# Turning part of the probability tiles by DMA in a two-layer attention trunk, with three score banks and a reordered gate projection

## The chip, the cores and the metric

The kernel runs on one core of one Trainium2 chip. The metric is device time in microseconds (us) of one execution. The profile and the trace are of one profiled execution.

## The reference: what is computed

Two layers on x of 1024 tokens by 1024 features, all in float32. Each layer normalises x, multiplies it with one wide input matrix whose columns hold all queries, keys, values and gates, runs two kinds of attention, multiplies each output with silu of its gate, and adds a final projection to x.

- Layer 1: attention A (8 heads, 2 key groups) sees the 256 keys that a separate small score picks for each query; attention B (8 heads, 2 key groups) sees a window of 128 keys and a sink.
- Layer 2: attention C (8 heads, 2 key groups) is a gated sum of three attentions: over compressed keys, over selected blocks (all 16 blocks are taken at this length, so it is causal), and over a window of 512. Attention D (8 heads) has queries and keys from low-rank latents, and is causal.

```python
def layer_ab(x, ...):
    y = rms_norm(x, norm_g) @ w_in
    qa, ka, va, qi, ki, wi, za, qb, kb, vb, zb = split_cols(y, AB_SPLITS)
...
    mix = jnp.concatenate([oa * jax.nn.silu(za), ob * jax.nn.silu(zb)], axis=-1)
    return x + mix @ w_out
```

Layer 2 has the same shape with C and D in place of A and B.

## The kernel before, in words

**Stages.** Queries go in tiles of 128 rows. The order of the stages, with their place in the profiled execution: normalising, first projections and the small scores (0 to about 165 us); a search in 2 x 16 steps for each query's threshold on VectorE, ScalarE and GpSimd (`topk`, L868), with the jobs of attention B beside it (to about 445); attention A (to about 600); the output projection of layer 1, normalising, and the first projections of layer 2 (to about 800); attention C, first key group 0, then 1, with the other projections beside it (to about 1215); keys and values of D, then attention D, key group 0, then 1, and the output tiles (to the end).

**Numbers.** Projections and scores are made as sums of products of a high and a low part (three or two matmuls each). Probabilities are also split: a high and a low 16-bit part.

**A job** (`attn_gen`, L617) is one query tile, one key group (4 heads) and, in C, one of three kinds. It is done in **units**: a unit is one pass over 4 heads when there are up to 2 key tiles, 2 heads for 3 or 4 key tiles, and 1 head for more. For each unit:
1. scores on TensorE into a PSUM bank `psS` (L665); the masked minimum of the negative on VectorE into `pt` (L668), the bias on ScalarE (L672), and the exponential with its sum on ScalarE (L674). `pt` has three buffers.
2. The probabilities must be turned (keys to partitions) before they can be multiplied with the values. The tiles of a unit are taken in groups of up to four. How a group is turned is given by a letter that cycles through `WAYS` (L73), with one entry for each kind of attention and key group. **p**: TensorE turns the tiles into a bank `psT` (L709), ScalarE copies the high part out (L712), VectorE subtracts for the low part (L713). **q**: the same turn, ScalarE copies all into `sg` (L716), and GpSimd makes both parts (L717, L718). **g**: ScalarE copies `pt` to 16 bits into `hl` (L693), GpSimd subtracts (L694), and a DMA transpose on SP's queue turns both halves at once into `ht` (L696); TensorE has no turn to do. Before, only B uses "g".
3. Three matmuls for each tile with the values, into the bank `psO` (L725 to L727). After a job's last group, `fin` scales the sum and stores it (L788 and L791, or L1337 to L1344 for C).

**The order of the work.** The turning stage and the value stage are closures in two queues, `tq` and `cq`. After the scores of a unit are written out, turning stages are taken from `tq` until only `tlag` of them (L782: the number of groups in this unit) are left, and a value stage is taken from `cq` when there is more than one.
Projections run beside the jobs: `Lanes.run` (L152) adds up costs that the two generators yield, and hands out projection steps (`fill_gen`, L495) up to a ratio of the attention's cost. Chunks of projections go in the order of the strings `FAO` (layer 1) and `FOO` (layer 2); a chunk of queries waits at its gate (L484) until one of three query buffers is free. Shorter chains (normalising, rotating and turning of queries and keys) are posted and go one step at each tick; one of them at a time may hold a `psT` bank. On top of that order, a scheduler of the framework that models the engines' times puts the instructions of each engine in a queue, with waits in between.

**PSUM** has eight banks: two `pp` for projections, two `psS` for scores, three `psT` for turned tiles, one `psO`. **Buffers:** `hl` (the tag under which `sg` also goes) and `ht` have four each (L41, L42).

**SP's queue** issues all loads and stores, in order, the DMA transposes among them.

## Time and profile before

| what | value |
|---|---|
| median of 3 runs | 1537.46 us (1534.99 to 1539.63) |
| profiled execution | 1541.3 us |
| its span, first to last instruction | 1539.1 us |
| mean granted TensorE clock | 0.950 |
| TensorE busy | 1355.2 us (88%) |
| VectorE busy | 1126.2 us (73%) |
| ScalarE busy | 940.5 us (61%) |
| GpSimd busy | 856.1 us (56%) |
| DMA, share of 16 engines | 22.9% |

In the rows, PE is TensorE (PEld its weight loads, which overlap its matmuls), DVE is VectorE, ACT is ScalarE, POOL is GpSimd, SP is SyncE. L709 is line 709 of the kernel. A busy share is an average over stages with different limits, so rows are read by stretch.

### The profile page before, as it was taken

To read this page: it belongs to the slowest core of one execution; us is meant where nothing else is said; L and a number is where in the kernel's file an instruction comes from. 1 tells how busy PE (TensorE), PEld (TensorE's weight loads), DVE (VectorE), ACT (ScalarE), POOL (GpSimd) and SP (SyncE) were. 2 spreads that over 40 slices of the span, in tenths; PEclk is the share of its full clock that TensorE was granted. 3 is DMA by queue.
4 is the path that set the end of the run, shared out by engine and by line. 5 is a ranking of instruction groups with operands and counts; after the bars stand their busy time and mean duration, and the time that the engine had idled before them with its cause. 6 is when DMAs were issued, how large, how long until landed. Compare 5 with 4: busy or idle time off the path is not lost.

```text
span 1539.1 us, 34696 instructions
## 1 busy us (share of the span) xinstructions
PE 1355.2 (88%) x12468; PEld 1244.8 (81%) x12468; DVE 1126.2 (73%) x3401; ACT 940.5 (61%) x2683; POOL 856.1 (56%) x1158
## 2 busy tenths in 40 slices
PE   5998899796268899999999999999998678789999
PEld 5997889695266788999999988899987557678887
DVE  5387888888888774185276678776699999986763
ACT  5355588788668763164246668747677677655541
POOL 6799549987466584225355334465455465742240
PEclk9999999998579999999899999999999879989999
DMA  6311373331131433142212110111100120111232
GB/s 201 91 30 34 73 143 78 75 63 52 35 101 47 111 92 112 44 157 61 54 29 79 46 29 6 29 53 49 33 7 30 59 61 14 35 62 63 93 114 76
DMA packets 120236, 100.83 MB, mean 66 GB/s; under 512 B 52992, under 2 KB 104960, under 8 KB 120064
## 3 DMA queue, kind: packets, MB, share of 16 engines
q1 hardware_dynamic: 120064, 98.62, 22.9%
q8 instruction: 98, 1.61, 0.4%
q14 instruction: 74, 0.61, 0.1%
HBM read 67.65 MB, written 23.07 MB: 59 GB/s over the span
## 4 chain that ended last, share of the span: by engine, by line
PE 49%; DVE 23%; ACT 9%; DMA 7%; POOL 6%; issue 6%; SPq 1%; POOLq 0%; DVEq 0%; ACTq 0%
PE pp L519 8%; PE pp L521 8%; PE pp L520 8%; PE psS L665 6%; PE psT L709 5%; DVE pt L668 4%; ACT pt L674 3%; ACT junka L885 2%; DMA wraw<-in_ab_w_in 2%; PE pp L1732 2%; PE pp L1734 2%; PE pp L1733 2%; DVE ht L713 1%; DVE junk L889 1%; PE po L727 1%
## 5 line engine op out<-in xcount | busy, mean ns | idle before, releaser
L519 PE MATMUL pp<-whi,Rh 128*128 128x256 f32 (+4 forms) x1648 | 480.4, 292 | 15.5 <-DVE zst L610 6.2
L521 PE MATMUL pp<-whi,Rl 128*128 128x256 f32 (+4 forms) x1648 | 475.5, 289 | 0.0
L520 PE MATMUL pp<-wlo,Rh 128*128 128x256 f32 (+4 forms) x1648 | 473.8, 288 | 1.1 <-POOL wlo L476 1.1
L519 PEld LDWEIGHTS pp<-whi,Rh 128*128 128x128 f32 x1648 | 315.5, 192 | 21.9 <-DVE zst L610 6.6
L520 PEld LDWEIGHTS pp<-wlo,Rh 128*128 128x128 f32 x1648 | 316.0, 192 | 3.1 <-POOL wlo L476 1.6
L521 PEld LDWEIGHTS pp<-whi,Rl 128*128 128x128 f32 x1648 | 315.6, 192 | 1.3
L674 ACT ACTIVATE pt<-pt,nm 128x256 f32<-128x256 f32 (+8 forms) x384 | 244.3, 638 | 3.5
L476 POOL TENSOR_TENSOR wlo<-wraw,whi 128x256 fp32r<-128x256 f32 (+4 forms) x208 | 162.8, 792 | 137.8 <-ACT whi L475 136.8
L709 PE MATMUL psT<-identf,pt 128*128 128x128 f32 x1136 | 195.9, 284 | 13.3 <-ACT pt L674 3.5
L475 ACT ACTIVATE whi<-wraw 128x256 fp32r<-128x256 f32 (+4 forms) x208 | 83.3, 416 | 134.7 <-DMA wraw<-in_ab_w_in 41.0
L709 PEld LDWEIGHTS psT<-identf,pt 128*128 128x128 f32 x1136 | 131.9, 143 | 28.0 <-ACT pt L674 8.5
L717 POOL TENSOR_SCALAR ht<-sg 128x512 f16<-128x512 f32 (+3 forms) x127 | 70.0, 552 | 142.0 <-ACT sg L716 108.5
L712 ACT ACTIVATE ht<-psT 128x512 f16<-128x512 f32 (+3 forms) x233 | 112.5, 493 | 57.2 <-PE psT L709 50.5
L713 DVE TENSOR_TENSOR ht<-psT,ht 128x512 f16<-128x512 f32 (+3 forms) x233 | 128.4, 558 | 18.3 <-ACT ht L712 17.4
L725 PEld LDWEIGHTS <-ht 128*128 128x128 f16 x1256 | 117.0, 100 | 26.2 <-DMA ht<-hl 8.4
L727 PEld LDWEIGHTS <-ht 128*128 128x128 f16 x1256 | 115.5, 100 | 26.8 <-POOL ht L718 8.8
L718 POOL TENSOR_TENSOR ht<-sg,ht 128x512 f16<-128x512 f32 (+3 forms) x127 | 127.3, 1003 | 7.2
L668 DVE CUSTOM_DVE_ANT_0 pt<-psS,mk 128x512 f32<-128x512 f32 (+4 forms) x208 | 107.5, 521 | 28.7 <-PE psS L665 22.7
L726 PEld LDWEIGHTS <-ht 128*128 128x128 f16 x1256 | 117.3, 100 | 2.1 <-issue 0.9
L672 ACT ACTIVATE nm<-nm 128x1 f32<-128x1 f32 (+2 forms) x208 | 41.9, 202 | 100.6 <-DVE nm L668 99.8
L716 ACT ACTIVATE sg<-psT 128x512 f32<-128x512 f32 (+3 forms) x127 | 66.7, 526 | 27.7 <-PE psT L709 26.7
L1093 POOL TENSOR_TENSOR mo<-mo,nz 128x256 f32<-128x256 f32 (+1 forms) x32 | 32.4, 1012 | 78.6 <-DMA nz<-zdr 49.6
(314 smaller groups left out, 3695.2 us busy)
## 6 DMA issues: line engine op xcount, KB each, us to landing
wraw<-in_cd_w_in SPq DMA_DIRECT2D x72, 128.0 KB, 2.1
wraw<-in_ab_w_in SPq DMA_DIRECT2D x56, 128.0 KB, 2.3
xs<-in_x SPq DMA_DIRECT2D x8, 512.0 KB, 6.2
od<-mx SPq DMA_DIRECT2D x32, 128.0 KB, 1.8
wraw<-in_ab_w_out SPq DMA_DIRECT2D x32, 128.0 KB, 2.2
x<-in_x SPq DMA_DIRECT2D x8, 512.0 KB, 5.0
mo<-od SPq DMA_DIRECT2D x16, 256.0 KB, 2.8
nz<-zdr SPq DMA_DIRECT2D x16, 256.0 KB, 3.0
```

What stands on the lines that cost most here:

```text
L476: G.tensor_tensor(lo[:, :o], raw[:, :o], hi[:, :o].bitcast(F32), OP.subtract)
L519: T.matmul(ps, xh, hi[:, :n], start=q == 0 and k == 0, stop=False)
L520: T.matmul(ps, xh, lo[:, :n], start=False, stop=False)
L521: T.matmul(ps, xl, hi[:, :n], start=False, stop=q == 3 and k == 1)
L668: V.tensor_tensor_reduce(pt[:, j * nk + c:j * nk + c + w], ps[:, at:at + w], mask(c, w), -1.0, first, op0=OP.add, op1=OP.min, accum_out=low)
L674: S.activation(pt[:, j * nk:(j + 1) * nk], pt[:, j * nk:(j + 1) * nk], AF.Exp, scale=-1.0, bias=nm[:, h:h + 1], accum_out=sm[:, h:h + 1])
L709: T.transpose(pT[:, a], pt[:, o:o + P], identf)
L713: V.tensor_tensor(pl, pT[:, :n], ph, OP.subtract)
L718: G.tensor_tensor(pl, sg[:, :n], ph, OP.subtract)
L725: T.matmul(dst, ph[:, a], vh(kt, h), start=kt == 0, stop=False)
L726: T.matmul(dst, ph[:, a], vl(kt, h), start=False, stop=False)
L727: T.matmul(dst, pl[:, a], vh(kt, h), start=False, stop=kt == nt - 1)
```

## The change

- In jobs of C's selected and windowed kinds and of D, the first group of up to four tiles of every unit but the job's last is turned by DMA, with a new letter "l": the split of "g", with its values multiplied not in its own turn but after the values of the next unit of the job. Such a group has no turning stage in `tq`.
- The other groups of C and D all go the way "p" (before: "ppq", "pq", "ppq" and "p").
- Tiles that TensorE turns go to a buffer of their own, `hp`, with four buffers; `hl` and `ht` have two each.
- The start and stop flags of the value matmuls are set once for the whole output bank, by a count, in place of once a head.
- Three banks for scores and two for turned tiles.
- The gate projection `z2` comes ahead of both chunks of A's (masked) queries.

```diff
-HLB = 4
-HTB = 4
+HLB = 2
+HTB = 2
+HPB = 4
...
-FAO = 'ki qi kb qb0 z0 z1 qb1 ka qa0 z2 qa1'
+FAO = 'ki qi kb qb0 z0 z1 qb1 ka z2 qa0 qa1'
...
-WAYS = ('g', 'g', 'ppq', 'pq', 'ppq', 'pq', 'ppq', 'p')
+WAYS = ('g', 'g', 'ppq', 'pq', 'p', 'p', 'p', 'p')
...
-    psA = {n: ctx.enter_context(tc.tile_pool(name=n, bufs=2, space=PSUM)) for n in ("pp", "psS")}
-    psT = ctx.enter_context(tc.tile_pool(name="psT", bufs=3, space=PSUM))
+    psA = {n: ctx.enter_context(tc.tile_pool(name=n, bufs=2, space=PSUM)) for n in ("pp",)}
+    psA["psS"] = ctx.enter_context(tc.tile_pool(name="psS", bufs=3, space=PSUM))
+    psT = ctx.enter_context(tc.tile_pool(name="psT", bufs=2, space=PSUM))
...
+            heads = [0]
+
+            def values(grp, ph, pl, get_po=get_po, heads=heads, nk=nk, vh=vh, vl=vl, cmp_=cmp_):
+                po = get_po()
+                nt = max(1, nk // P)
+                for a, (h, kt, o) in enumerate(grp):
+                    dst = po[:, h:h + 2].rearrange("p h d -> p (h d)") if cmp_ else po[:, h]
+                    T.matmul(dst, ph[:, a], vh(kt, h), start=heads[0] == 0, stop=False)
+                    T.matmul(dst, ph[:, a], vl(kt, h), start=False, stop=False)
+                    heads[0] += 1
+                    T.matmul(dst, pl[:, a], vh(kt, h), start=False, stop=heads[0] == (2 if cmp_ else 4 * nt))
...
+                u += 1
                 for c in range(0, len(todo), 4):
                     n = min(4, len(todo) - c)
-                    way.append(next(jb["way"]))
+
+                    way.append("l" if c == 0 and jb.get("late") and h0 + per < 4 else next(jb["way"]))
                     ht = None
-                    if way[-1] in "dg":
+                    if way[-1] in "dgl":
...
+                    if way[-1] == "l":
+                        late.append((u, lambda values=values, g=todo[:n], ht=ht, n=n: values(g, ht[:, :n], ht[:, n:2 * n])))
                     turned.append(ht)
                 for c in range(0, len(todo), 4):
+                    if way[c // 4] == "l":
+                        continue
...
                         if way in "pq":
-                            ht = wk.tile([P, 8, P], F16, name="ht", bufs=HTB)
+                            ht = wk.tile([P, 8, P], F16, name="hp", bufs=HPB)
...
+                            values(grp, ph, pl)
+                            k = n
+                            while endu and late and late[0][0] < u:
+                                late.pop(0)[1]()
+                                k += 4
+                            if endu and fb is not None:
                                 assert fb
-                                fin(po, fb[0])
-                            return n * 87 + (0 if not lastg else 1)
+                                fin(get_po(), fb[0])
+                            return k * 87 + (0 if not endu else 1)
```

## Rows read from the trace of the kernel before

**Rows 1.** Busy time by stretch: start:end length, engines, clock, DMA share, GB/s
```profile
350.00:445.00 95.00, 42.40 (x320) 37.62 (x319) 78.80 (x189) 60.73 (x149) 54.95 (x52) 0.64 0.25 63
445.00:600.00 155.00, 138.01 (x1636) 119.06 (x1635) 113.98 (x325) 115.81 (x300) 101.12 (x128) 1.00 0.31 92
900.00:1000.00 100.00, 93.73 (x1088) 82.23 (x1089) 81.32 (x303) 74.96 (x233) 41.52 (x57) 0.98 0.05 15
1000.00:1100.00 100.00, 99.85 (x1023) 97.34 (x1022) 67.93 (x243) 61.38 (x204) 55.44 (x75) 1.00 0.16 46
1100.00:1245.00 145.00, 116.16 (x1217) 101.70 (x1216) 133.85 (x541) 100.77 (x328) 83.65 (x125) 0.91 0.10 32
1245.00:1380.00 135.00, 108.44 (x976) 93.37 (x975) 126.99 (x385) 93.29 (x255) 81.77 (x104) 0.92 0.15 47
1380.00:1524.00 144.00, 143.81 (x1155) 121.48 (x1155) 94.04 (x268) 66.35 (x174) 39.13 (x50) 1.00 0.26 85
```

**Rows 2.** Chain of waits by line: 850-1000, 1100-1245, 1380-1524, 1245-1380
```profile
by line: PE psT L709 13.7%; PE psS L665 11.9%; ACT pt L674 10.4%; PE pp L520 7.0%; PE pp L521 7.0%; PE pp L519 6.9%; issue 6.7%; DVE pt L668 4.6%; DMA wraw<-in_cd_w_in 4.2%; PE po L727 3.4%; PE po L725 3.2%; PE po L726 3.1%; DVE ht L713 2.4
...
by line: DVE pt L668 10.9%; ACT pt L674 6.9%; PE psT L709 6.7%; PE psS L665 5.3%; issue 4.5%; DVE kd L1539 4.5%; DVE ht L713 4.4%; DVE rs_t L310 3.7%; DVE rs_t L312 2.7%; DVE rs_y L313 2.7%; DVE ydup L1436 2.5%; DVE rs_t L309 2.4%; DVE rs_t
...
by line: PE pp L1732 17.4%; PE pp L1734 16.8%; PE pp L1733 16.7%; PE psS L665 15.1%; PE psT L709 10.0%; PE psT L1100 3.2%; PE po L725 3.0%; PE po L727 2.9%; PE po L726 2.8%; PE psT L1669 1.9%; PE psT L1686 1.9%; DMA mo<-od 1.9%; PE psT L112
...
by line: DVE pt L668 13.7%; DVE ht L713 6.5%; PE psS L665 6.4%; DVE rs_v L306 4.3%; DVE qrs L1691 4.2%; issue 4.1%; PE psT L709 3.5%; DVE kd L1539 2.5%; ACT pt L674 2.5%; DVE nz L1654 2.3%; DVE rs_t L309 2.3%; DVE qhl L1673 2.3%; PE psT L16
```

**Rows 3.** Turns on TensorE: their group (busy, mean ns), a chain piece
```profile
L709 PE MATMUL psT<-identf,pt 128*128 128x128 f32 x1136 | 195.9, 284 | 13.3 <-ACT pt L674 3.5 <-DVE ht L713 2.5 <-ACT sg L716 2.2
...
941.88 1.09 PE psT L709 x8
```

**Rows 4.** Turned groups: L713, L716 from 1100 to 1245 (ns); then whole span
```profile
L713 DVE TENSOR_TENSOR ht<-psT,ht x34: 276/552/692, 1102.9 to 1213.7; 128x512 f16<-128x512 f32 x16, 128x128 f16<-128x128 f32 x12, 128x384 f16<-128x384 f32 x4, 128x256 f16<-128x256 f32 x2
...
L716 ACT ACTIVATE sg<-psT x34: 267/578/637, 1103.6 to 1212.3; 128x512 f32<-128x512 f32 x20, 128x128 f32<-128x128 f32 x8, 128x256 f32<-128x256 f32 x6
...
L717 POOL TENSOR_SCALAR ht<-sg 128x512 f16<-128x512 f32 (+3 forms) x127 | 70.0, 552 | 142.0 <-ACT sg L716 108.5 <-ACT nm L672 30.4 <-DVE ht L713 1.7
...
L718 POOL TENSOR_TENSOR ht<-sg,ht 128x512 f16<-128x512 f32 (+3 forms) x127 | 127.3, 1003 | 7.2
...
L693 ACT ACTIVATE hl<-pt 128x512 f16<-128x512 f32 x30 | 17.7, 619 | 0.0
...
L694 POOL TENSOR_TENSOR hl<-pt,hl x30: 1145/1167/3132, 182.7 to 434.6; 128x512 f16<-128x512 f32 x30
```

**Rows 5.** DMA transposes, L696: issue ns, who waited (us, times), landing
```profile
L696 SPq DMA_TRANSPOSE ht<-hl x30: 1231/1238/2548, 183.9 to 437.7; - x30
...
  PEld L725: 8.4, 11
...
DMA to landing us min/median/max: 3.0/3.3/4.8
```

**Rows 6.** One bias a unit, L672, from 900 to 1000
```profile
L672 ACT ACTIVATE nm<-nm x32: 185/198/205, 901.3 to 980.9; 128x1 f32<-128x1 f32 x20, 128x2 f32<-128x2 f32 x8, 128x4 f32<-128x4 f32 x4
```

**Rows 7.** SP's queue: what it waited for (us in total, times, longest)
```profile
SPq L1344 <- POOL cacc L1342: 157.6, 15, 27.6
```

**Rows 8.** Waits from 445 to 600: L709 (two rows), L665 (us, times)
```profile
  ACT sg L716: 4.4, 6
  DVE ht L713: 1.8, 6
...
  DVE nm L668: 6.9, 13
```

**Rows 9.** z2's posts, L610, 270 columns; TensorE's longest wait, 350 to 400
```profile
L610 DVE SCALAR_TENSOR_TENSOR zst<-zst,pp x6: 429/432/437, 332.2 to 349.3; 128x270 f32<-128x270 f32 x6
...
L610 DVE SCALAR_TENSOR_TENSOR zst<-zst,pp x2: 430/433/436, 351.4 to 355.4; 128x270 f32<-128x270 f32 x2
...
PEld psS L665 <- DVE nm L668: 28.0, 1, 28.0
```

More of the change, by code (lines that the diff above doesn't have):

```diff
@@ L617, in attn_gen @@
     def attn_gen(jobs):
-        tq, cq = [], []
+        tq, cq, late = [], [], []
         def do_T():
@@ L625, in do_C @@
             cq.pop(0)()
+        u = 0
         for jb in jobs:
@@ L1368, in job_c @@
         need = [("qc", g, i - i % 2)] + [[("cmp",)], [("ks", i - i % 2), ("vs", i)], [("kw", i - i % 2), ("vw", i)]][kind]
-        return dict(need=need, nk=nk, npass=2, start=start, norm=softmax_norm(mul), tlag=tlag, way=ways[4 + g],
+        return dict(need=need, nk=nk, npass=2, start=start, norm=softmax_norm(mul), tlag=tlag, late=kind > 0, way=ways[4 + g],
                     free=cfree if i % 2 and kind == 2 else None)
@@ L1720, in job_d @@
         need = [("qd", g, i)] + [(n, g, j) for j in range(0, i + 1, 2) for n in ("kd", "vd")]
-        return dict(need=need, nk=(i + 1) * P, npass=3, start=start, norm=softmax_norm(), tlag=tlag, way=ways[6 + g],
+        return dict(need=need, nk=(i + 1) * P, npass=3, start=start, norm=softmax_norm(), tlag=tlag, late=True, way=ways[6 + g],
                     cut=SEQ - 256 * g, free=lambda: [L.give(n) for n in ("qs", "qd")])
```

12 lines of the change are left out of this document (2 added, 10 removed).

## The prediction, made before the change was run

> **What bounds the kernel now.** I first cut the span into stretches and read the engines' busy shares [rows 1]. From 350 to 445 us the search for the largest scores keeps VectorE at 79 of 95 us while TensorE works 42. From 445 to 600 (attention A) TensorE is at 138 of 155. From 900 to 1000 (attention C, first key group, almost no projections beside it) TensorE is at 93.7 of 100, VectorE at 81.3. From 1000 to 1100 TensorE is full. Then it turns: from 1100 to 1245 (C's second group and the start of D) VectorE is at 133.9 of 145 and TensorE at 116, and from 1245 to 1380 (D's first group) 127 of 135 against 108. From 1380 to 1524 (D's second group with the output tiles) TensorE is at 143.8 of 144.
>
> Second, the chain of waits in those stretches [rows 2]: from 850 to 1000 the turning of probability tiles on TensorE (L709) is its largest line, 13.7%; from 1100 to 1245 the masked minimum on VectorE (L668) leads and L709 has 6.7%; from 1380 to 1524 projections, scores and L709 (10.0%) stand one behind the other, all on TensorE. So a turn taken off TensorE is worth its price from 850 to 1100 and from 1380 on, and little in between.
>
> **The change, part by part.** Late groups. A unit (one pass over 1, 2 or 4 heads of a job) that isn't the last of its job hands its first four tiles to the DMA. In C's selected and windowed kinds and in D, a job of 3 or 4 key tiles has two units, one of 5 or more has four. That is 1+1+4x3 = 14 groups for each of six (kind, key group) pairs: 84 groups, 336 of the 1136 turns. On the chain eight turns in a row take 1.09 us [rows 3], 0.136 us each, so 0.544 us a group and 45.7 us in all. The three value matmuls a tile stay, and the flags of their first and last cost nothing.
>
> By stretch, from the order of jobs: 28 groups lie from 850 to 1000 (15.2 us), 4 from 1000 to 1100 (2.2), 24 from 1100 to 1245, 14 from 1245 to 1380, 14 from 1380 on (7.6).
> - 850 to 1000: all 15.2 us would press the hundred us near its end to about 87, with 79 of VectorE's work in it, 90%; where VectorE binds now it is at 92 to 94%. So it nearly fits; I take 12.
> - 1000 to 1100: 2.2. 1380 on: 7.6, since VectorE has 94 of 144 there.
> - 1100 to 1380: what VectorE gains or loses. A one-tile subtraction out of PSUM takes 0.276 us, a four-tile one 0.692 [rows 4], so 0.14 a group and 0.138 a tile. From 1100 to 1245 the cycle "pq" put 34 groups (92 tiles) on VectorE and 34 on GpSimd. All of the 44 groups left now go to VectorE with 96 tiles: 19.4 us against 17.5, 1.9 lost. In D's first group, 29 groups keep about 88 tiles in place of 97: 1.3 gained. TensorE's clock is granted at 0.92 there, and at 0.64 from 350 to 445, where it is busy 45% [rows 1]. Were it to fall as far with 7.6 us of turns gone, (108 x 0.92 - 7.6) / 0.64 = 143 us of TensorE would stand in 135: up to 8 lost, nothing taken.
>
> Sum of the gains: 12 + 2.2 + 7.6 - 1.9 + 1.3 = 21.2 us.
>
> What a late group adds. ScalarE copies it to 16 bits in 0.62 us and GpSimd subtracts in 1.17 (L693, L694), where ScalarE's copy out of PSUM took 0.58 and the GpSimd way 0.55 + 1.00 (L717, L718) [rows 4]. In C and D 92 GpSimd groups (about 143 us) go and 84 subtractions (98 us) come: ScalarE is even, GpSimd lighter, and neither binds there [rows 1]. SP spends 1.24 us on the issue, and the tile lands 3.3 us after it begins (at most 4.8) [rows 5].
>
> Is it there in time? It is multiplied with the next unit's values. As two turned groups now make the lag of the queue, and a late unit has one, that is some four units behind its own scores. But only two tiles can be turned at once, and the third waits until the first is multiplied: that leaves two units. From 901 to 981 us there are 32 units [rows 6], 2.6 us each, so 5.1 us against 3.3 and the wake-ups. It fits with about 1.5 us to spare. Behind it on SP stand weight loads and result stores; in front may stand a store that waits for GpSimd's sum: 15 such waits, 157.6 us [rows 7]. Costed from both sides: nothing, or what the DMA-turned groups of B pay now, 8.4 us over 30 [rows 5], 0.28 each, 23.5 for 84. B's are multiplied one unit behind, these with up to four, so I take the value near nothing: 4 us lost.
>
> Banks. Three for scores, two for turned tiles, one of which a projection's own transposes may hold. In C and D fewer groups need them. A keeps all its turns: with three banks TensorE's two queues waited there 6.2 us for a bank's evacuation, and 6.9 for a score bank [rows 8]. One bank less may double or triple the former (6 to 12 lost), one more may remove most of the latter (up to 7 gained). Between +7 and -12 I take 3 us lost.
>
> Buffers. B's turned and split tiles go from four to two, a job needs two: the next job's DMA waits for this one's values, but TensorE reaches those right behind the next scores. From nothing to 8.4 us again; 2 lost. A's 35 GpSimd groups get two staging tiles instead of four, one group in 4.4 us (155/35), each held about 2.5: inside A's term.
>
> The gate projection. z2 (8 x 24 matmuls) is written ahead of qa0. But it already ran at 332 to 355 us, and TensorE then stood 28 us in front of a score bank that VectorE had no time for [rows 9]. Its loads, tanh and store come earlier on SP, ScalarE and VectorE, behind nothing that is short there. Nothing, and if it pushes the search, 8 x 0.43 us on VectorE, 3.5; if it fills TensorE's idle time instead, as much gained.
>
> Pacing. A late group yields no turning cost, so 28 x 440 ns x 0.75 = 9 us less of projections are handed out beside C's second group. They stay in a stretch that VectorE bounds: nothing; without that cover, 9 us.
>
> Net: 21.2 - 4 - 3 - 2 = 12.2 us faster. The profiled execution took 1541.3 us (span 1539.1, 2.2 around it), 3.8 above the median of 1537.46. The sum on its own time gives 1529.1; on the median 1525.
>
> One rule speaks against this. The tile's eight 128x128 blocks land together in 3.3 us, 0.41 a block, beside 0.136 for a turn on TensorE [rows 3, 5]. The Trainium skill, in "VectorE: DVE Perf Modes", section "The three transpose paths", puts a 128x128 16-bit transpose at 390 ns on TensorE and 1309 by DMA, and its rules for authors advise TensorE where PSUM will do as the destination. Worked out from that page, an estimate: eight blocks take 10.5 us, 5 more than the two units, and C and D come out slower. The trace disagrees on the number, and the measurement decides; the direction is that of the first rival, which has its price from rows.
>
> **The rivals.**
> 1. The turned tile comes late (slower). Place: L725 of a late group, TensorE in order behind it; SP's queue holds the DMA behind a store or a load. B's eleven waits last 0.76 us each. From 22 of the 84 groups waiting so (16.2/0.76, the sum without its 4 us for this), the kernel is slower. At B's rate (31 of 84, 23.5 us) the time is 1537.5 - 16.2 + 23.5 = 1545; at two of three (42.6 us), 1564. For it: 1.5 us of room, and SP's long waits. Against: at most 4.8 us to landing, DMA engines busy 5% there.
> 2. VectorE takes over at once (no change). From 850 to 1000 the score and subtraction chain, not TensorE's time, sets the pace: its 12 are gone, and 9.2 against 9 lost leave 1537. For it: VectorE at 81% with 10.4% of the chain in the exponentials that it feeds. Against: TensorE at 94%.
> 3. More than the sum. From 1100 to 1380 the turns on the chain go too: 6.7% of 145 us, 9.7, and in D's first group 3.5% of 135, 4.7 [rows 2], and the losses stay away: 1537.5 - 21.2 - 14.4 = 1502. For it: turning two units behind removes TensorE's waits for exponentials. Against: VectorE above 92%.
>
> **How the numbers follow.** Forecast 0.50, rival 1 0.24, rival 2 0.14, rival 3 0.12. A measurement of this kernel can tell about 0.3%, 4.6 us, from no change. The forecast's own range is 1512 to 1534: faster 0.47, same 0.03. Rival 3 is all faster, rival 2 is 0.02 faster, 0.09 same, 0.03 slower, rival 1 0.02 same and 0.22 slower. Faster 0.61, same 0.14, slower 0.25. The range reaches down to rival 3 and up into rival 1, 1500 to 1552, leaving out rival 1's upper half and what lies below rival 3.
>
> **What would show it.** L709 1136 to 800 matmuls; L716 to L718 from 127 to 35; L693, L694 and the DMA transposes from 30 to 114; L713 241 groups. C's stretch with TensorE bound shorter by some 14 us, 1100 to 1380 unchanged with VectorE above 92%, D's end shorter by 7 us, A longer by some 3. TensorE's waits at the value matmuls for the DMA should total under 10 us. I am wrong if these exceed 20 us, if A grows by more than 10, or if VectorE's share from 850 to 1000 reaches 92% with TensorE waiting on score banks.

## The result, and the profile after

The changed kernel takes 1548.97 us (median; 1544.12 to 1556.83); the kernel before, run beside it on the same chip, takes 1538.73. The ratio is 1.0075 [1.0056, 1.0095]: some 11 us slower, where 12 us faster was forecast. The profiled execution took 1544.7 us (span 1542.9).

First the changed kernel's page: the engines' busy time over the span, and the groups of the turned tiles (busy, mean ns, idle before).

```profile
PE 1342.5 (87%) x12132; PEld 1222.8 (79%) x12132; DVE 1104.0 (72%) x3409; ACT 943.3 (61%) x2683; POOL 817.6 (53%) x1058
...
L731 PE MATMUL psT<-identf,pt 128*128 128x128 f32 x800 | 142.9, 287 | 23.5 <-DVE hp L735 11.6 <-ACT sg L738 4.2 <-DVE qs L400 2.7
L712 POOL TENSOR_TENSOR hl<-pt,hl 128x512 f16<-128x512 f32 x114 | 137.3, 1209 | 143.1 <-ACT hl L711 98.1 <-ACT nm L688 12.7 <-issue 12.4
L735 DVE TENSOR_TENSOR hp<-psT,hp 128x512 f16<-128x512 f32 (+3 forms) x241 | 124.1, 520 | 19.4 <-ACT hp L734 18.6
```

The counts came as forecast: 800 turns on TensorE for 1136, 114 split groups, 241 of VectorE's. The turns' busy time fell by 53 us [rows 3]; TensorE's idle time in front of them rose from 13.3 to 23.5 us. Every engine but ScalarE has less to do, and the kernel is slower.

The same stretches as in [rows 1], of the changed kernel (columns as there: busy us of PE, PEld, DVE, ACT, POOL, then the granted TensorE clock, DMA share, GB/s):

```profile
350.00:445.00 95.00, 53.28 (x440) 47.88 (x438) 78.30 (x174) 58.22 (x160) 75.00 (x69) 0.71 0.24 61
445.00:600.00 155.00, 131.34 (x1435) 110.54 (x1434) 100.46 (x290) 104.65 (x258) 93.79 (x118) 0.96 0.28 85
900.00:1000.00 100.00, 89.78 (x1009) 78.78 (x1008) 76.86 (x310) 72.92 (x227) 34.22 (x38) 1.00 0.32 66
1100.00:1245.00 145.00, 112.14 (x1090) 93.35 (x1089) 125.75 (x542) 100.00 (x319) 63.85 (x81) 0.86 0.36 74
1245.00:1380.00 135.00, 101.19 (x889) 85.30 (x888) 124.97 (x388) 90.77 (x252) 75.13 (x89) 0.90 0.32 73
1380.00:1524.00 144.00, 138.08 (x1090) 114.27 (x1089) 84.87 (x240) 66.23 (x169) 54.24 (x64) 1.00 0.40 106
```

From 445 to 600 us, most of attention A, TensorE ran 1435 matmuls, before 1636. From 1245 to 1380 it ran 889 for 976, and from 1380 on it is no longer full, 138.08 of 144 against 143.81.

Where each stage ends is read from TensorE's matmuls by tile: the last two columns of times are the first and the last start. `ki` are the search's scores, `vhb` the values of B, `vha` those of A, `kd` D's scores. First before, then after:

```profile
L844 PE MATMUL psS<-ki,qs x80: 222/391/568, 79.3 to 163.2; 128*128 128x512 f32 x48, 128*128 128x384 f32 x16, 128*128 128x128 f32 x8, 128*128 128x256 f32 x8
...
L727 PE MATMUL po<-vha,ht x288: 192/193/206, 445.6 to 595.0; 128*128 128x64 f16 x144
...
L727 PE MATMUL po<-vhb,ht x120: 193/193/242, 187.4 to 441.4; 128*128 128x64 f16 x120
```

```profile
L864 PE MATMUL psS<-ki,qs x80: 223/392/497, 76.0 to 139.0; 128*128 128x512 f32 x48, 128*128 128x384 f32 x16, 128*128 128x128 f32 x8, 128*128 128x256 f32 x8
...
L664 PE MATMUL po<-vhb,ht x120: 193/193/242, 174.4 to 428.0; 128*128 128x64 f16 x120
...
L664 PE MATMUL po<-vha,hp x288: 191/193/277, 433.3 to 606.3; 128*128 128x64 f16 x144
...
L681 PE MATMUL psS<-kd,qhl x192: 222/389/795, 1237.8 to 1509.8; 128*128 128x512 f32 x72, 128*128 128x256 f32 x48, 128*128 128x320 f32 x32, 128*128 128x384 f32 x24
```

The scores of the search end 24 us earlier and B 13 us earlier; then A takes 25 us longer (from B's end to A's, 153.6 before, 178.3 after), and ends 11 us later. The stretch from there to C's first score is 8 us shorter (210 to 202), so C starts only 3 us later. C is shorter (410 us from first score to last values before, 387 after), the step to D's first score gives 15 back (27 to 43), and D takes 283 us for 278. D's last values come at 1521 us in both; the 4 us by which the spans differ lie behind them, where more of the output tiles' projections are left.

The same reading for every kernel of this study, from its own profile, in us from the span's start. A stage ends with the end of its last matmul, some 0.2 us behind its last start. A profiled execution can lie several us off its kernel's median: that of the kernel before (1541.3 us) is 3 to 6 us above the medians that it has beside the others (1535.1 to 1538.7), that of the changed kernel 4 us below its own, that of x3_late 7 below. So times are judged by the ratio (each with the kernel before beside it), and these columns show only the place:

| kernel (label) | ratio [95%] | B ends | A ends | C's first score | C's last values | D's first score | D's last values | span |
|---|---|---|---|---|---|---|---|---|
| before | 1 | 442 | 595 | 805 | 1216 | 1243 | 1521 | 1539 |
| changed | 1.0075 [1.0056, 1.0095] | 428 | 606 | 808 | 1195 | 1238 | 1521 | 1543 |
| x1_order | 1.0043 [1.0028, 1.0057] | 444 | 602 | 807 | 1219 | 1245 | 1521 | 1539 |
| x2_banks | 1.0266 [1.0244, 1.0288] | 426 | 605 | 810 | 1232 | 1255 | 1553 | 1575 |
| x3_late | 0.9971 [0.9954, 0.9988] | 441 | 595 | 801 | 1189 | 1235 | 1502 | 1524 |
| x4_nobanks | 1.0012 [0.9996, 1.0028] | 445 | 601 | 808 | 1198 | 1244 | 1511 | 1533 |
| y1_turned2 | 1.0296 [1.0278, 1.0313] | 442 | 620 | 822 | 1242 | 1267 | 1557 | 1579 |
| y3_pace | 0.9933 [0.9912, 0.9953] | 444 | 598 | 807 | 1211 | 1237 | 1508 | 1526 |
| x5_noorder | 1.0150 [1.0125, 1.0174] | 427 | 607 | 811 | 1199 | 1243 | 1532 | 1554 |
| y4_shared | 1.0097 [1.0078, 1.0117] | 424 | 597 | 802 | 1206 | 1262 | 1524 | 1544 |
| z1_after_pace | 1.0062 [1.0037, 1.0087] | 428 | 605 | 810 | 1216 | 1242 | 1522 | 1544 |
| z2_lateC_pace | 0.9952 [0.9934, 0.9971] | 445 | 598 | 804 | 1210 | 1236 | 1512 | 1530 |
| z3_pace_pq | 1.0052 [1.0032, 1.0071] | 451 | 604 | 809 | 1228 | 1252 | 1526 | 1544 |
| z4_banks_order | 1.0198 [1.0176, 1.0221] | 431 | 605 | 809 | 1231 | 1255 | 1546 | 1568 |
| x6_p_only | 0.9982 [0.9963, 1.0000] | 439 | 593 | 802 | 1212 | 1239 | 1514 | 1532 |
| s0_before_search3 | 0.9983 [0.9965, 1.0001] | 435 | 591 | 801 | 1211 | 1238 | 1516 | 1534 |
| s3_search3 | 0.9921 [0.9900, 0.9942] | 433 | 586 | 793 | 1185 | 1229 | 1499 | 1521 |
| s1_search3_pace | 0.9875 [0.9853, 0.9898] | 437 | 591 | 798 | 1204 | 1228 | 1499 | 1517 |
| u1_ht3 | 0.9900 [0.9879, 0.9922] | 435 | 597 | 804 | 1208 | 1233 | 1505 | 1523 |
| u2_hl3_ht3 | 0.9930 [0.9912, 0.9947] | 433 | 609 | 810 | 1212 | 1235 | 1503 | 1522 |

### The profile page after: what moved, and what is told of

It reads as the page before. It is cut to its first block, busy times and chain, and to the rows that moved or that the text cites. A ratio compares the mean times of both kernels' runs of the same rounds, so it can differ in the third digit from the quotient of the medians.

```text
span 1542.9 us, 34205 instructions
## 1 busy us (share of the span) xinstructions
PE 1342.5 (87%) x12132; PEld 1222.8 (79%) x12132; DVE 1104.0 (72%) x3409; ACT 943.3 (61%) x2683; POOL 817.6 (53%) x1058
## 3 DMA queue, kind: packets, MB, share of 16 engines
q1 hardware_dynamic: 208768, 120.65, 31.1%
## 5 line engine op out<-in xcount | busy, mean ns | idle before, releaser
L521 PE MATMUL pp<-whi,Rh 128*128 128x256 f32 (+4 forms) x1648 | 480.0, 292 | 23.2 <-DVE tgt L937 4.9
L521 PEld LDWEIGHTS pp<-whi,Rh 128*128 128x128 f32 x1648 | 315.6, 192 | 29.7 <-issue 8.0
L712 POOL TENSOR_TENSOR hl<-pt,hl 128x512 f16<-128x512 f32 x114 | 137.3, 1209 | 143.1 <-ACT hl L711 98.1
L731 PE MATMUL psT<-identf,pt 128*128 128x128 f32 x800 | 142.9, 287 | 23.5 <-DVE hp L735 11.6
L734 ACT ACTIVATE hp<-psT 128x512 f16<-128x512 f32 (+3 forms) x241 | 108.4, 460 | 76.0 <-PE psT L731 71.6
L735 DVE TENSOR_TENSOR hp<-psT,hp 128x512 f16<-128x512 f32 (+3 forms) x241 | 124.1, 520 | 19.4 <-ACT hp L734 18.6
L731 PEld LDWEIGHTS psT<-identf,pt 128*128 128x128 f32 x800 | 93.9, 145 | 35.4 <-DVE hp L735 10.9
L661 PEld LDWEIGHTS <-hp 128*128 128x128 f16 x800 | 76.0, 100 | 24.1 <-ACT hp L734 6.0
L664 PEld LDWEIGHTS <-hp 128*128 128x128 f16 x800 | 74.1, 100 | 22.5 <-DVE hp L735 12.4
L711 ACT ACTIVATE hl<-pt 128x512 f16<-128x512 f32 x114 | 71.1, 626 | 17.9 <-DMA ht<-hl 17.0
L662 PEld LDWEIGHTS <-hp 128*128 128x128 f16 x800 | 75.7, 100 | 5.8 <-issue 4.9
L1362 POOL TENSOR_TENSOR cacc<-cacc 128x256 f32<-128x256 f32 x32 | 24.0, 749 | 97.6 <-DVE cacc L1357 62.1
L690 ACT ACTIVATION_READ_ACCUMULATOR pt<-pt,nm 128x1 f32 x384 | 72.8, 190 | 0.0
```

What stands on the lines that cost most here:

```text
L521: T.matmul(ps, xh, hi[:, :n], start=q == 0 and k == 0, stop=False)
L661: T.matmul(dst, ph[:, a], vh(kt, h), start=heads[0] == 0, stop=False)
L690: S.activation(pt[:, j * nk:(j + 1) * nk], pt[:, j * nk:(j + 1) * nk], AF.Exp, scale=-1.0, bias=nm[:, h:h + 1], accum_out=sm[:, h:h + 1])
L712: (V if way[-1] == "d" else G).tensor_tensor(hl[:, w:], pt[:, o:o + w], hl[:, :w], OP.subtract)
L731: T.transpose(pT[:, a], pt[:, o:o + P], identf)
L734: S.activation(ph, pT[:, :n], AF.Copy)
```

## The experiments

### The three parts, each alone

**x1_order**: the kernel before with z2 in front of qa0.
```diff
-FAO = 'ki qi kb qb0 z0 z1 qb1 ka qa0 z2 qa1'
+FAO = 'ki qi kb qb0 z0 z1 qb1 ka z2 qa0 qa1'
```


> The kernel before with one part of the change: the gate projection z2 ahead of both chunks of A's queries. Theory 1 (the changed order is what ate the gain: in the changed kernel the masks are done 14 us earlier and A starts 25 us earlier, but ends 11 us later, with GpSimd blocked some 10 us on a constant's load): A's scores start some 20 us earlier here too, A ends 5 to 12 us later, and the time is 3 to 10 us above before. Theory 2 (the banks ate it): A is unchanged and the time is within 4 us of before.

**x2_banks**: the kernel before with the new banks.
```diff
-    psA = {n: ... bufs=2 ... for n in ("pp", "psS")}
-    psT = ... name="psT", bufs=3 ...
+    psA = {n: ... bufs=2 ... for n in ("pp",)}
+    psA["psS"] = ... name="psS", bufs=3 ...
+    psT = ... name="psT", bufs=2 ...
```


> The kernel before with one part of the change: three banks for scores, two for turned tiles. Theory 2 (two turned banks hold up A, which still turns all its tiles on TensorE): A's stretch grows by 10 to 20 us and the time by 8 to 20 us; waits of TensorE's turns for evacuation at least double from 6.2 us. Theory 1 (order): within 4 us of before.

**x3_late**: the change without those two edits (late groups, ways, buffers).


> The kernel before with one part of the change: first groups of C and D turned by DMA with the new ways and buffers, banks and order as before. My prediction's sum for this part alone is 12 to 17 us faster (C 14 or more, the end 7, less waits). Theory 3 (what C gains is given back where keys of D are made and in D, as the changed kernel's milestones show: C 23 us shorter, then 15 us longer to D's first score, D 5 us longer): within 5 us of before.

**x4_nobanks**: the change without the bank edit alone.


> The changed kernel with the banks of before (two for scores, three for turned tiles). Theory 2: at least 10 us faster than the changed kernel, so at or below before. Theory 1: as slow as the changed kernel, within 4 us. Theory 3: C's stretch and D's keep the lengths of the changed kernel.

Measured: order 1.0043, banks 1.0266, late groups 0.9971; late groups with the order 1.0012. So 41 us are lost by the banks alone, 7 by the order, and 4.5 gained by the late groups. The bank edit is the largest loss. Added last, to late groups and order, it costs 1.0075 - 1.0012 = 0.0063, 9.7 us. The table shows two opposite effects in it: x2 has B's end 16 us earlier and A 26 us longer, D 20 longer.

Of the theories on record: the time of x1_order (7 us) and A's end (6.5 us later) lie where theory 1 has them, but A's scores start at 429 us for 427 before, not 20 us earlier; in x2_banks they start at 401, so A's early start comes with the banks. x2_banks loses more than theory 2's 8 to 20 us, and x4_nobanks is 9.7 us under the changed kernel, close to its 10. x3_late is within theory 3's 5 us and not at the 12 to 17 that the prediction's sum gives; its D is shorter, though, not longer.

Where the 9.7 us lie shows between x4_nobanks and the changed kernel, whose profiles are 10 us apart. B ends 16.5 us earlier, A is 21.5 longer and the stretch behind it 4.5 shorter, so C's first score comes at 808 us in both: up to there the bank edit costs nothing. C and the step to D are 7 us shorter. D takes 283 us for 267, and that is the loss. D in x4_nobanks, then in the changed kernel (columns as above), and its turns on TensorE (last the idle time before them):

```profile
1244.00:1511.00 267.00, 240.04 (x1994) 201.20 (x1993) 207.32 (x637) 160.71 (x431) 133.27 (x156) 0.94 0.37 95
...
L730 PE MATMUL psT<-identf,pt 128*128 128x128 f32 x176 | 31.8, 295 | 1.6 <-ACT pt L689 0.6 <-DVE hp L734 0.5 <-ACT kd L1557 0.4
```
```profile
1238.00:1521.00 283.00, 242.36 (x1993) 201.88 (x1991) 213.47 (x638) 161.23 (x432) 134.41 (x156) 0.95 0.36 90
...
L731 PE MATMUL psT<-identf,pt 128*128 128x128 f32 x176 | 32.4, 299 | 10.5 <-DVE hp L735 8.9 <-DVE qrs L1711 1.3 <-DVE rs L784 0.3
```

The matmuls and the clock are the same; TensorE stands idle for 40.6 us in place of 27.0. In front of its turns the idle time grows from 1.6 to 10.5 us, 8.9 of it until VectorE's subtraction (L735) has read a turned bank. Beside the late groups alone (x3_late to x5_noorder) it is the same: D from 267 to 289 us, that idle time from 1.4 to 14.8; there C's first score comes 10 us later as well.

### Which of the two bank edits

**y1_turned2**: one turned bank less, nobody gets it.
```diff
-    psT = ctx.enter_context(tc.tile_pool(name="psT", bufs=3, space=PSUM))
+    psT = ctx.enter_context(tc.tile_pool(name="psT", bufs=2, space=PSUM))
```


> The kernel before with two banks for turned tiles and two for scores; one bank is given to nobody. All of the reference is computed. Theory 2a (the lost third turned bank is the whole price of the bank change, and the third score bank is a gain that gives some 15 us back in the search): attention A about 25 us longer than in the kernel before (178 against 154), D about 20 longer, the search (B's last values at 441.6 us) not earlier; the whole 15 us or so above the run with both bank edits, that is 1585 to 1595. Rival 2b (the third score bank does the harm: scores run ahead of the turns and take TensorE from them): A at 154 to 158 and the whole within 10 us of the kernel before. In between, 1560 to 1580: both have a part.

Measured 1.0296, A 178 us long, D 289, B's end where it was. A is as theory 2a has it; D is 11 us longer than in the kernel before, not 20, and the whole is 0.0030 above x2, 5 us, not 15. So the lost turned bank is the price, but of the 16 us that the third score bank gains in the search only 5 are left at the end: 8 go again in D (289 us here, 298 in x2).

What the third turned bank does in A. The waits of 430 to 625 us (who waited for whom: us in total, times, longest), first of the kernel before, then of y1_turned2, then of the changed kernel:

```profile
DVE pt L668 <- PE psT L709: 13.2, 11, 2.0
...
ACT sg L716 <- PE psT L709: 6.2, 11, 2.2
```
```profile
DVE pt L668 <- PE psT L709: 23.7, 23, 3.1
ACT sg L716 <- PE psT L709: 17.4, 21, 2.2
```
```profile
DVE pt L684 <- PE psT L731: 23.7, 22, 2.4
ACT sg L738 <- PE psT L731: 15.8, 18, 2.0
```

VectorE, which needs a free `pt` and gets it when one has been turned, and ScalarE, which copies the turned tiles, wait for a turn twice as often. One of the two banks may be held by a projection's transposes: 3.4 us of the second row below end with the read of such a bank (L398). TensorE's own wait in front of its turns is small (the groups by line in A, last number the idle time before; first before, then y1_turned2):

```profile
L709 PE MATMUL psT<-identf,pt 128*128 128x128 f32 x288 | 47.3, 281 | 3.2 <-ACT sg L716 1.9 <-ACT whi L475 0.4 <-ACT pt L674 0.2
```
```profile
L709 PE MATMUL psT<-identf,pt 128*128 128x128 f32 x288 | 50.0, 293 | 7.0 <-DVE qs L398 3.4 <-ACT sg L716 2.2 <-DVE ht L713 1.4
```

And the whole of A in both, with 25 us stretches of it (the same columns as above):

```profile
490.00:515.00 25.00, 21.54 (x292) 18.09 (x288) 20.86 (x61) 20.73 (x48) 11.11 (x13) 1.00 0.33 106
515.00:540.00 25.00, 20.59 (x219) 17.23 (x218) 17.16 (x55) 18.73 (x57) 15.05 (x23) 1.00 0.39 89
...
441.00:595.00 154.00, 139.67 (x1645) 120.39 (x1643) 114.11 (x329) 117.99 (x309) 101.68 (x127) 0.99 0.30 88
```
```profile
465.00:490.00 25.00, 20.75 (x237) 16.98 (x234) 17.60 (x54) 16.73 (x45) 17.98 (x27) 0.86 0.14 46
...
515.00:540.00 25.00, 18.89 (x180) 14.96 (x180) 15.26 (x50) 16.38 (x51) 9.16 (x15) 0.81 0.25 52
...
441.00:620.00 179.00, 156.07 (x1674) 131.91 (x1674) 117.34 (x335) 121.61 (x311) 103.97 (x129) 0.94 0.26 81
```

TensorE's idle time rises from 14.3 to 22.9 us, 8.6. The other 16.4 of A's 25 us are busy time: 1674 matmuls take 156.07 us where 1645 took 139.67. These are not the same matmuls. One of the three projection lines in A, before and then y1_turned2 (L520 and L521 go from 72 each to 81 each):

```profile
L519 PE MATMUL pp<-whi,Rh 128*128 128x256 f32 x73 | 21.4, 293 | 0.2 <-ACT sq L453 0.2
```
```profile
L519 PE MATMUL pp<-whi,Rh 128*128 128x256 f32 x82 | 24.9, 303 | 1.9 <-DVE x L1141 1.1 <-ACT sq L453 0.6 <-ACT Rh L355 0.3
```

So 27 more projection matmuls stand in the longer A; the three lines take 72.6 us for 62.9, 9.7 of the 16.4. That work comes out of the stretch behind A, which is 8 us shorter (202 us for 210): C's first score is 17 us later than before, not 25. The other 6.7 us are all else, taking longer. The clock is granted at 0.94 of 2.4 GHz in the mean over A, for 0.99 before, and is lowest, 0.81, from 515 to 540 us; 179 x 0.06 - 154 x 0.01 = 9.2 us of full clock not granted, an estimate that counts idle time too, so it can cover those 6.7 us. Behind A, C is 10 us longer than in the kernel before, D 11 and the rest 4.

**y4_shared**: late groups with one ring of five banks for scores and turned tiles.
```diff
+    psA["psS"] = psT = ctx.enter_context(tc.tile_pool(name="psST", bufs=5, space=PSUM))
...
-        return psT.tile([P, 4, P], F32, name="psT")
+        return psT.tile([P, 4, P], F32, name="psT", tag="b5")
...
```


> The late groups alone (old order), with the scores' two banks and the turned tiles' three put into one ring of five that both take from in the order of the program. Theory 2c (both users only need a bank often enough, the search more of them for scores and A and D more of them for turned tiles): the search ends as early as with three score banks (426 to 430 us against 441), A and D stay at 154 and 267, and the whole is 1520 to 1525. Rival 2d (in one ring a tile waits for whichever older tile holds the next bank, so a turned tile waits for the evacuation of scores by a busy VectorE and the other way round): A or D over 10 us longer, the whole 1540 or more.

Measured 1.0097: theory 2c fell. The search is as early as hoped (424), but A takes 173 us, 19 longer, as rival 2d has it, and ends at 597, no earlier than without the shared ring. The step from C to D is 56 us.

### The order beside the banks

**x5_noorder**: the change with the old `FAO`.


> The change without its order part: late groups and the new banks, the old order of the gate projection. If the parts add up (order alone +6 us, order beside the late groups +5): 1543, A and the search 3 us shorter than in the changed kernel. Rival (the order was there for the new banks, and with three score banks it costs nothing or pays): 1549 or more.

**z4_banks_order**: banks and order, no late groups.


> The new banks and the new order, without the late groups: the one combination not run. Without the late groups, the banks alone gave 1.0266 and the order alone 1.0043; beside the late groups the order took 11 us off the new banks (1.015 to 1.0075). If order and banks act on each other whatever the late groups do: 1.018 to 1.021. If they only add: 1.029 to 1.033.

Measured 1.0150 and 1.0198, so the parts don't add up, and order and banks act on each other. The order costs 0.0043 alone and 0.0041 beside the late groups (x3 to x4), but gains 0.0068 beside the banks (x2 to z4) and 0.0075 in the change (x5 to the changed kernel), whatever the late groups do. From x2 to z4 all 7 us by which the profiles differ lie in D, far behind the edit; from x5 to the changed kernel it is 5.5 of 11. D in x2, then in z4:

```profile
1255.00:1553.00 298.00, 264.81 (x2108) 220.51 (x2109) 225.03 (x657) 163.50 (x435) 123.11 (x156) 0.92 0.18 61
```
```profile
1255.00:1546.00 291.00, 256.21 (x2106) 212.84 (x2105) 221.87 (x653) 162.61 (x432) 121.46 (x155) 0.95 0.19 61
```

The work is the same; TensorE's busy time and its granted clock differ (298 x 0.08 - 291 x 0.05 = 9.3 us of full clock not granted, an estimate as above). Why the order of a gate projection in layer 1 should move D's clock was not found.

### The late groups: pacing, place and ways

**y3_pace**: late groups alone, and a late group hands out as much of the projections as four turns.
```diff
                     if way[-1] == "l":
                         late.append(...)
+                        yield n * 110
```


> The late groups alone (old banks, old order), with one edit more: a late group hands the projections beside it the time of four turns, as a group turned on TensorE does. Theory 3a (the step from C's last values to D's first score grew from 27 to 46 us because less of the projections was handed out beside C, and the rest had to be done at its end): the step goes back to 27 to 35, and C's own length grows by less than that; the whole 5 to 10 us under the run with the late groups alone, 1523 to 1528. Rival 3b (that stretch is VectorE's: what C gains, VectorE's work for D's keys gives back, whoever is handed what): the step shrinks by as much as C grows, and the whole stays at 1530 to 1535.

**z1_after_pace**: the same line in the changed kernel.


> The changed kernel with one line more: a late group hands the projections the time of four turns. If the pacing is what the late groups lose (the line took the late groups alone from 0.9971 of the kernel before to 0.9933), the step from C's last values to D's first score falls from 42.6 us to some 25 to 30, and the whole lies 5 to 8 us under the changed kernel: a ratio of 1.002 to 1.004. Rival (that line's gain belongs to the old banks, or is chance between runs): the step may move, the ratio stays at 1.006 to 1.009.

The step from C's last values to D's first score, in the kernel before, the changed kernel and y3_pace:

```profile
1216.00:1243.00 27.00, 11.33 (x52) 9.01 (x51) 25.35 (x85) 16.08 (x47) 14.64 (x16) 0.66 0.14 45
```
```profile
1195.00:1238.00 43.00, 24.96 (x98) 19.83 (x95) 40.29 (x156) 25.53 (x82) 22.83 (x27) 0.58 0.17 53
```
```profile
1211.00:1237.00 26.00, 11.50 (x53) 9.21 (x51) 24.73 (x82) 14.65 (x43) 14.14 (x16) 0.64 0.15 48
```

Of C's gain of 23 us in the changed kernel 15 come back as a longer step, in which VectorE is busy for 40 of 43 us with 156 instructions where there were 85: work for D's keys that was not handed out beside C. The line on pacing moves it back into C. With the late groups, the step and C together stay the same within 5 us (from C's first score to D's: 430 changed, 433 with the line; 434 in x3, 430 in y3; 438 in the kernel before). In the changed kernel the line is worth nothing that can be told (1.0075 to 1.0062). On the old banks it took the ratio from 0.9971 to 0.9933, in theory 3a's range, and in the last pair below from 0.9921 to 0.9875. Where those 6 to 7 us come from the profiles don't show: they place the pairs within 4 us of each other.

**z2_lateC_pace**: y3_pace with late groups in C alone, and the old cycle of ways in D.


> Old banks, old order, late groups in C alone with the line on pacing; D as in the kernel before, every group turned on TensorE with its old cycle of ways. Tells what D's late groups are worth. If they gave D its 8 to 11 us (D's first score to last values 278 before, 267 to 271 with them): D back at 276 to 280 and a ratio of 0.998 to 1.001. Rival (the gain is C's alone, D's length is chance): D at 268 to 272 and the ratio at 0.993 to 0.995.

Measured 0.9952, D 276 us long: D's late groups are worth 0.0019 (3 us) by the medians, and some 5 us of D's length (276 for 271 in y3). The intervals overlap, and the two signs on record point to different theories: D's length to late groups that pay there, the ratio to a gain that is C's alone.

**x6_p_only**: only the ways.
```diff
-WAYS = ('g', 'g', 'ppq', 'pq', 'ppq', 'pq', 'ppq', 'p')
+WAYS = ('g', 'g', 'ppq', 'pq', 'p', 'p', 'p', 'p')
```


> Of the late part only the ways: no late groups, old buffers, banks and order, but C's second key group and D's first have VectorE subtract for every group that TensorE turns, where VectorE and GpSimd took turns. Keeping the old ways beside the late groups cost 1.2% (1.0052 against 0.9933). Theory 4a (the gain belongs to the late groups, the ways only make room on GpSimd for their subtractions): alone the ways add some 17 to 20 us of VectorE work to a stretch that VectorE bounds, and C and D grow together by 5 to 15 us: 1.003 to 1.010. Rival 4b (GpSimd's slow subtraction held up the queue of turned tiles all along, and the DMA's turns bring nothing): 0.990 to 0.996.

**z3_pace_pq**: y3_pace with the old cycle in C's second group and D's first.


> The late groups with the line on pacing (0.9933), old banks and order, but C's second key group and D's first keep the old cycle in which groups that TensorE turns are split by VectorE and GpSimd by turns. If VectorE sets the pace from 1100 to 1380 us: C's second group and D's first shorter by 3 to 8 us together, a ratio of 0.989 to 0.992. Rival (GpSimd, which now subtracts for the late groups in the same stretch, makes the turned groups late): C or D longer, a ratio of 0.996 or more.

The ways alone: 0.9982, close to nothing; neither 4a's loss nor 4b's gain. Beside the late groups they are needed: with the old cycle 1.0052 against 0.9933, 18 us, and 15 of them lie in C's second group. That stage, in y3_pace, then in z3_pace_pq:

```profile
1010.00:1211.00 201.00, 182.10 (x1969) 166.20 (x1968) 164.72 (x695) 138.98 (x470) 77.28 (x104) 0.97 0.35 75
```
```profile
1012.00:1228.00 216.00, 193.58 (x1967) 174.78 (x1966) 164.62 (x679) 140.91 (x473) 104.91 (x148) 0.91 0.31 70
```

GpSimd has 28 us more to do, as the rival had it. TensorE's idle time grows by little (18.9 to 22.4 us); the same number of matmuls takes 11.5 us longer, at a clock of 0.91 for 0.97 (216 x 0.09 - 201 x 0.03 = 13.4 us of full clock not granted).

### The search's third bank, without the loss

**s0_before_search3, s1_search3_pace, s3_search3**: every third score tile of the search takes a bank of the turned tiles, in the kernel before, in y3_pace and in x3_late.
```diff
...
-                        ps = bank("psS")
+                        m += 1
+                        ps = bank("psS") if m % 3 else tps().rearrange("p a n -> p (a n)")
```


> The kernel before with nothing but the borrowed bank for the search's scores. If the gain of that edit is its own: the search ends 8 to 15 us earlier and the whole 8 to 12 us, a ratio of 0.992 to 0.995. Rival: 0.998 to 1.002.

> The late groups with the line on pacing (0.9933), old banks and order; and every third score tile of the search takes its bank from the turned tiles' three, which attention hardly uses then. A third score bank for that part alone, without the loss of a turned bank in A and D. If the search's earlier end (426 to 430 us against 441 to 446 in all runs with three score banks) comes from its scores and not from attention's: B's last values at 428 to 434, A's length unchanged at 154 to 158, the whole at 1510 to 1518, a ratio of 0.983 to 0.989. Rival (it comes from the attention B beside it, or is given back in A): within 0.3% of 0.9933.

> The same without the line on pacing. That line is for the third time alone between two kernels: it took the late groups from 0.9971 to 0.9933, and the changed kernel from 1.0075 to 1.0062, a step inside the intervals. If it is worth 5 us: 0.3 to 0.5% above the run with it. If nothing: equal within 0.2%.

Measured 0.9983 [0.9965, 1.0001], 0.9875 and 0.9921. So s1_search3_pace is 1.25% faster than the kernel before (1516.9 us) and beats both. Its search scores and A, by tile and in one stretch:

```profile
L866 PE MATMUL psS<-ki,qs x54: 222/394/497, 77.9 to 139.8; 128*128 128x512 f32 x32, 128*128 128x384 f32 x12, 128*128 128x128 f32 x6, 128*128 128x256 f32 x4
...
L868 ACT ACTIVATE r<-psT x13: 277/587/604, 79.5 to 140.5; 128x512 f32<-128x512 f32 x8, 128x384 f32<-128x384 f32 x2, 128x256 f32<-128x256 f32 x2, 128x128 f32<-128x128 f32 x1
```
```profile
437.00:591.00 154.00, 141.39 (x1640) 125.12 (x1639) 111.69 (x328) 117.26 (x310) 103.21 (x129) 0.97 0.31 93
```

The scores end at 140 us, as with three score banks (139), and A keeps its 154 us. B ends 7 us earlier than in y3_pace (437 for 444), most of the 8 us by which the two profiles differ; a third score bank of its own gave 13 to 17 (table), and where the rest of that comes from was not tried. Beside the late groups the borrowed bank is worth 0.0058 and 0.0050, 8 to 9 us; on the kernel before, 0.0017 [-0.0001, 0.0035], as the rival has it and less than the 8 to 12 us of the other theory.

### Is it the two buffers?

**u1_ht3**, **u2_hl3_ht3**: s1_search3_pace with other numbers of buffers.
```diff
-HLB = 2
-HTB = 2
-HPB = 4
+HLB = 2
+HTB = 3
+HPB = 3
```
(u2_hl3_ht3: 3, 3, 2.)

> The fastest so far (late groups, line on pacing, borrowed bank for the search's scores: 0.9875) with three buffers for tiles turned by DMA instead of two, and three instead of four for those turned on TensorE. In the late groups with pacing, the chain of waits from 850 to 1000 us has the DMA transposes as its largest line, 13.5%, the place that the turns on TensorE had before with 13.7%. If the two buffers make it so (a third tile's transpose can't start until the first is multiplied): that line falls under 8%, C's first key group is 3 to 6 us shorter, and the ratio is 0.983 to 0.986. Rival (the transposes are there because a late group is multiplied one unit after its own, whatever the buffers): the ratio stays at 0.986 to 0.990.

> The same with three buffers also for the 16-bit copies that the DMA reads, and two for the tiles turned on TensorE. If ScalarE's waits for such a copy to be read (10.8 us in C and D of the changed kernel) hold the DMA transposes back: 0.2 to 0.4% under the run with three turned buffers alone. Rival (two buffers for the tiles turned on TensorE delay A's and D's turned groups by more than that): over 0.990.

Measured 0.9900 and 0.9930. The chain of waits from 850 to 1000 us in y3_pace, s1_search3_pace and u1_ht3:

```profile
by line: DMA ht<-hl 13.5%; issue 8.7%; ACT pt L689 8.3%; PE pp L520 7.9%; PE pp L522 7.7%; PE pp L521 7.6%; PE psS L680 5.8%; DMA wraw<-in_cd_w_in 4.9%; DVE pt L683 4.5%; POOL hl L711 3.9%; ACT hp L734 2.8%; PE psT L731 2.7%; ACT hl L710 2.
```
```profile
by line: ACT pt L689 11.6%; DMA ht<-hl 11.1%; issue 8.0%; PE pp L520 7.7%; PE pp L522 7.3%; PE pp L521 7.1%; DVE pt L683 5.8%; PE psS L680 4.5%; POOL hl L711 3.9%; DMA wraw<-in_cd_w_in 3.4%; PE psT L731 3.2%; ACT hp L734 3.1%; ACT hl L710 3
```
```profile
by line: DMA ht<-hl 13.3%; ACT pt L689 9.4%; PE pp L520 9.1%; PE pp L522 8.9%; PE pp L521 8.6%; PE psS L680 7.0%; issue 7.0%; DMA wraw<-in_cd_w_in 5.4%; DVE pt L683 3.7%; POOL hl L711 3.1%; PE psT L731 3.0%; DVE hp L735 2.9%; ACT hl L710 2.
```

The turns' share of the chain fell from 13.7% to 2.7% [rows 2], and the DMA's transposes took that place. A place on the chain is no wait of that length: the chain counts the whole transfer that it passes through, even where only its end was waited for. A third turned buffer doesn't change it (13.3%), and C's first key group is 204 us long for 203: that theory fell. With a third copy buffer as well (u2_hl3_ht3) the time is no better. Both ratios are where the rivals on record have them. What the other side of the exchange goes with shows in A: with four, three and two buffers for the tiles turned on TensorE it takes 154, 162 and 176 us (from B's end to A's). The other buffers of these kernels differ too, but they only grow.

## Why the prediction was wrong

The forecast was a gain of 15.2 us by the late groups (21.2 - 4 - 2), nothing by the order and 3 lost by the banks. Added one after another the parts measured 4.5 gained (x3_late), 6.3 lost (x4_nobanks) and 9.7 lost (the changed kernel). So the 23.7 us between forecast and result are 10.7 of the late groups, 6.3 of the order and 6.7 of the banks, and no one term explains the sign. With the parts added in another way the shares differ: without the order the banks cost 28, and the order then pays 11.

**Banks: a step that failed, for D above all.** "Between +7 and -12 I take 3 us lost" was sized by TensorE's waits in A. Beside the other two parts the banks cost 9.7 us, beside the late groups alone 0.0179, 28 us, and alone 41. Three things were wrong. First, "in C and D fewer groups need them" put D at nothing. D takes 283 us in the changed kernel for 267 in x4_nobanks, with 13.7 us more of idle TensorE and 10.5 for 1.6 in front of its turns; up to C's first score the bank edit cost nothing. Second, TensorE's waits for a bank are not the price of a bank even in A: with one turned bank less its idle time there rose by 8.6 us, inside the forecast's 6 to 12, but A grew by 25, with projections that came in from the stretch behind it (8 us shorter) and at a lower clock. Third, the gain of a third score bank was looked for in A, whose score-bank waits stayed (5.3 us before, 5.1 after, in front of the scores' weight loads), and is in the search, 13 us, which the prediction didn't name. The sign "I am wrong if A grows by more than 10" came true, though the gain in the search and the shorter stretch behind A pay for that growth to 3 us.

**The gate projection: "nothing", with 3.5 us either way.** It costs 7 us alone and pays 11 beside the banks. Both lie outside the bounds; the reason is open.

**Late groups: right in direction, too large; the step that missed most.** The forecast had 15.2 us net. Measured by the medians: 4.5 us [1.8, 7.1], and 10.3 [7.2, 13.5] with the line on pacing. The term that failed is C's: 12 and 2.2 gained, 1.9 lost. Changed kernel: C's first key group is 8.5 us shorter (207.8 to 199.3, from C's first score to the second group's), the second group and the step to D 0.6 longer, 7.9 gained for 12.3. In x3_late C itself is 22 us shorter, but the step 19 longer, 3.4 gained for 12.3: the work for D's keys that C no longer covers comes back, on VectorE. D came near its 8.9: in x3_late it is 11 us shorter, of which 3.4 come back behind D's last values, where more output projections are left. (The profiles of x3_late and of the kernel before differ by 15 us, the medians by a third of that; some 10 us of what they show by place is the two executions' own.) In the first group the press on VectorE to 90% didn't come: 900 to 1000 has TensorE at 89.8, VectorE at 76.9 and neither full. The chain there (y3_pace) has the DMA where the turn was.

**Waits for the DMA: right.** The waits at the value matmuls of C and D, in the changed kernel from 800 to 1000, then from 1100 to 1245 (none from 1000 to 1100 and behind 1245):

```profile
PEld L661 <- DMA ht<-hl: 1.7, 3, 0.9
PE po L661 <- DMA ht<-hl: 1.4, 2, 0.8
```
```profile
PEld L661 <- DMA ht<-hl: 4.5, 7, 1.5
PE po L661 <- DMA ht<-hl: 3.2, 7, 1.3
```

10 of the 84 late groups were waited for, 6.2 us in all, forecast 4, for the 22 from which rival 1 would decide. So rival 1, which gave 1545 us, came near the time measured by luck, for a reason that isn't there. By the prices that the prediction took from the Trainium skill ("VectorE: DVE Perf Modes", section "The three transpose paths") C would have come out slower; it came out shorter, 387 us for 410.

**Pacing: "nothing, without that cover 9 us".** Right in the changed kernel, where the line makes no difference that can be told. On the old banks it is worth 6 to 7 us.

**Ways and buffers.** 0.6 us lost by the ways was forecast; alone they are 0.9982 [0.9963, 1.0000], the same. The buffers' 2 us can't be told from the rest: in x3_late, which has the new buffers and the old banks, B ends at 441 us as before, and A takes the same 153.6 us, so its 35 GpSimd groups were not hurt by two staging tiles.

**Rival 2** (VectorE takes over) is not seen from 850 to 1000. **Rival 3** (1502) wanted another 14 us from 1100 to 1380, and no run shows them: without the bank and order edits and with the line on pacing the late groups give 10.3 us in all. The 1517 us of s1_search3_pace take 8 to 9 more from the search, which is no part of that rival.

## What to carry to other kernels

A buffer's worth isn't the producer's wait for it. With the bank edit TensorE's idle time in front of its turns in D rose by 9 us and D by 16; with one turned bank less, it waited 4 us more at its turns in A and A grew by 25. And a stage's length isn't its price: 8 of those 25 us were work taken from the stretch behind, so a stage is judged together with what follows it. Before resources are moved from one ring to another, try the ring that loses with nothing given to anyone; that run alone (1.0296) would have shown that the third turned bank has a price. And a bank that is idle in one stage can be lent for that stage in one line, without taking it from the next.

## What the runs showed of the hardware

- TensorE's granted clock was lower in some of the slower stages and not in others. From 515 to 540 us it was 1.00 with TensorE busy for 20.6 of 25 us in the kernel before, and 0.81 with 18.9 of 25 in y1_turned2; in the mean over A 0.99 and 0.94. In C's second group it was 0.97 and 0.91 (y3_pace, z3_pace_pq), where the same matmuls took 11.5 us longer, and in D 0.95 and 0.92 (z4_banks_order, x2_banks), where they took 8.6 us longer. But in D of x4_nobanks and of the changed kernel it was 0.94 and 0.95, with 13.7 us more of idle time in the second.
- The DMA transposes went from 30 to 114 and the DMA queue's share of its engines from 22.9% to 31.1%, and 10 of the 84 late groups were waited for, 6.2 us in all.
